# Head 0's attention operands over other tiles and through GpSimd's queue, one mLSTM stage queued behind head 0's exponentials, and a residual loaded by column range

## The chip, the cores and the metric

The kernel runs on one core of a Trainium2 chip. The profile names the core's engines: PE is TensorE (matmuls; PEld its weight loads), DVE is VectorE, ACT is ScalarE, POOL is GpSimd, and SP is SyncE, which here only issues DMAs. Each engine works through its own instructions in a fixed order, and semaphores tie the engines together: an instruction that waits holds up everything behind it on its engine. DMAs are issued from the queues of SP, ACT and POOL and run on 16 DMA engines that all queues share.

The metric is the device time of one execution in microseconds (us). A profiled execution gives a span, from the first instruction to the last, and the clock that TensorE was granted, as a share of full speed.

## The reference

The reference is one layer of a streaming encoder for a prompt of 1024 frames and a sample of 32 frames, with the same weights. All is float32. Cut to what matters here:

```python
h = x * (1 + sc1) + sh1                                  # adaLN from c
mq, mk, mv, mo, mi, mf, fq, fk, fv, ff, gu, gv = split(h @ w_in)
hm, state = mlstm(mq, mk * 64 ** -0.5, mv, mi, log_sigmoid(mf))   # 4 heads, 64-frame chunks
hm = head_norm(hm) * mlstm_norm_g * sigmoid(mo)
logits = fq @ fk.T * 64 ** -0.5 + F_q - F_k              # FoX, 8 heads, causal, F = cumsum(log_sigmoid(ff))
hf = softmax(logits) @ fv
hg = gu * (tril(ws) @ layer_norm(gv) + bs)               # gMLP over 128 frames
x = layer_norm(ALPHA * x + (1 + g1) * (concat(hm, hf, hg) @ w_o))
h = x * (1 + sc2) + sh2
y = (silu(h @ w_gate) * (h @ w_up)) @ w_down
x = layer_norm(ALPHA * x + (1 + g2) * y)
```

The outputs are x for both groups, the FoX keys, values and log forget values, the mLSTM states and the sample's gMLP rows.

## The kernel before

**Arithmetic.** A float32 product is made of three passes: each operand is split into a rounded part (hi) and the rest (lo), and TensorE adds hi x hi, hi x lo and lo x hi (`gemm`, lines 116 to 118 of the kernel). Weights come in units of 128 x 1024 by SyncE into one of three `raw` tiles (`weights`); ScalarE makes hi (line 104), VectorE makes lo (line 105).

**Stages.** Frames are columns. They are worked on in two groups, 0 to 511 and 512 to 1055 (the last 32 are the sample). First the input projections run, with the first group's share of FoX and mLSTM woven in; the results that the second group will need go out to DRAM (`dqh`, `dql` are the hi and lo parts of the scaled queries and of the keys). The region of this change follows:

1. `fm_unit` for heads 2 to 4 projects the second group's queries and keys; `evac_qk` splits them into the tiles qkh and qkl, keeps the plain keys in qkr, and stores all three.
2. `wo_mix` loads the first group's mixer outputs; `wo_res` loads the residual x of that group into the tile z0, eight row blocks of 512 columns, in four DMAs.
3. `wo_range` is the first group's output projection, once for columns 0 to 255 and once for 256 to 511, over eight weight units m. `sublayer_end` scales the result and adds the residual (line 1066); in this phase GpSimd first takes a pivot off z (line 1061). The second pass keeps the weights of the first, except m = 3 and 4. The tiles for m = 0, 1, 2 are in a pool of their own, `pw`, and m = 2 is the last of the second pass.
4. `ln1` normalises each range and writes the FFN's operand (tm_ah, tm_al); `fm_unit` for heads 5 to 7 runs beside it. For these three heads the key store leaves from ScalarE's queue.
5. `ln1_res` (line 1101, GpSimd) turns z into the FFN's residual, sixteen operations.
6. `mixers` is the second phase of FoX, for the second group's queries: for each head `fox` loads its operands (k1, k2, qp, q2 and v) and works through four tiles of 128 queries. A tile is scores (lines 779 and 780, in two PSUM banks), a mask and row maxima (782, 783), exponentials on ScalarE (788), and a scaling (796). Transposes and products with v follow (815, 823, 828). mLSTM's chunks 4 to 8 are woven in with heads 1 to 5, in stages; the first stage loads a chunk's operands and makes the output gate with three steps on ScalarE (607 to 609) and one on GpSimd (610).
7. The FFN of the first group follows in program order (`up`, `down`).

**What sets the order.** The program is traced in this order, and a planner then places each instruction on its engine by a model of the times, with earlier instructions first where several are ready. So FFN matmuls stand between the mixers' matmuls on TensorE. `issue_after(ins)` keeps instructions that are traced in its block, on the engine of `ins`, behind `ins` in that engine's order.

**Where tiles lie.** Pools opened on the right side stack downward from the top of the on-chip memory. In steps 1 to 5 the pools `p1` (the projections' operand h1 and some small tiles) and below it `sm` (the small working tiles of step 1 and earlier) stand there. They are closed before step 6, and the mixers' pool `mx1` takes the same room, beginning a little below where `sm` begins. A tile of `mx1` waits for whoever last used the tiles that it covers. In `sm` the tiles lie in the order traw, vhl, tmsum, qkr, qkh, qkl, some very small ones, gvn, gms; in `mx1` the order is k1 (two), k2, qp, q2, v, the row maxima, the probabilities, and the rest.

Of the kernel before, what the change touches and what calls it, by code (L numbers as in the profile page):

```python
# [15 lines left out]
P = 128  # L16
# [47 lines left out]
def f(ap):  # L64
    return ap.bitcast(F32)


class Kernel:
# [14 lines left out]

    def load(self, out, in_):
        self.lastload = self.nc.sync.dma_start(out, in_)
        return self.lastload
# [271 lines left out]
    def evac_qk(self, h, act=False):  # L358
        nc = self.nc

        def evac(o, n, ps):
            hi = self.t(self.sm, [P, 272], F32R, "qkh", 2)
            lo = self.t(self.sm, [P, 272], F32R, "qkl", 2)
            kr = self.t(self.sm, [P, 272], F32, "qkr", 2)
            nc.scalar.activation(hi[:, :n], ps, AF.Copy, scale=self.qsc)
            nc.vector.scalar_tensor_tensor(lo[:, :n], ps, self.qsc, f(hi[:, :n]), ALU.mult, ALU.subtract)
            if act:
                nc.scalar.activation(kr[64:, :n], ps[64:], AF.Copy)
            else:
                nc.gpsimd.tensor_tensor(kr[:, :n], f(hi[:, :n]), f(lo[:, :n]), ALU.add)  # L370
            self.store(self.dqh[h, :, o:o + n], f(hi[:, :n]))
            self.store(self.dql[h, :, o:o + n], f(lo[:, :n]))
            self.store(self.d["o_kT"][h, :, o:o + n], kr[64:, :n], nc.scalar if act else nc.gpsimd)
            if o + n == T:
                if act:
                    nc.scalar.activation(self.qks[:, h, :], ps[:, n - NS:], AF.Copy, scale=self.qsc)
                else:
                    nc.gpsimd.tensor_copy(self.qks[:, h, :], kr[:, n - NS:n])
        return evac

    def decay(self, out, h, rows, tiles):
        j0, j1 = tiles
        self.load(f(out).rearrange("p (j q) -> p j q", q=P),
                  self.dfs.rearrange("(j h) r q -> h r j q", h=8)[h, rows, j0:j1])

# [6 lines left out]
    def head_unit(self, h):  # L392
# [17 lines left out]
        for o in (0, 256):  # L410
            kr = self.t(self.sm, [P, 272], F32, "qkr", 2)
            nc.scalar.copy(kr[hi, :256], ps[hi, o:o + 256])
# [11 lines left out]
    def evac_mqk(self, i, scale):  # L424
        nc = self.nc

        def evac(o, n, ps):
            r = self.t(self.sm, [P, 272], F32, "qkr", 2)
            nc.scalar.activation(r[:, :n], ps, AF.Copy, scale=scale)
# [307 lines left out]
    def fox(self, h, chunks):  # L737
# [6 lines left out]
        else:  # L744
            k1, k2, qp, q2, v = self.head_tiles(h, nq, nk)
            qs = slice(q0, q1)
            self.load(f(qp[0:64]), self.dqh[h, 0:64, qs])
            self.load(f(qp[64:128]), self.dql[h, 0:64, qs])
            self.load(f(k1[0:64]), self.dqh[h, 64:128, :nk])
            self.load(f(k1[64:128]), self.dqh[h, 64:128, :nk])  # L750
            self.load(f(q2[0:64]), self.dqh[h, 0:64, qs])
            self.decay(q2[64:68], h, slice(2, 6), (chunks[0][0], nb))
            self.load(f(k2[0:64]), self.dql[h, 64:128, :nk])
            self.decay(k2[64:68], h, slice(0, 4), (0, nb))
            self.load(f(v), self.dv[:, :nb, h * P:(h + 1) * P])
# [5 lines left out]
    def fox_chunk(self, h, tiles, W, nq, k1, k2, qp, q2, v):  # L761
# [5 lines left out]
        for i in tiles:  # L767
# [19 lines left out]
            for x, (lo, hi) in enumerate(cuts):  # L787
                nc.scalar.activation(pr[:, lo:hi], banks[x][:, :hi - lo], AF.Exp, bias=mxs[:, 0:1],  # L788
                                     accum_out=sums[:, x:x + 1])
            if len(cuts) > 1:  # L790
# [222 lines left out]

    def wo_res(self, c, pool):
        z = self.z[c] = self.t(pool, [P, KT, GN[c]], F32, f"z{c}", 1)
        for k in range(0, KT, 2):
            self.load(z[:, k:k + 2], self.d["xT"][k:k + 2, :, GO[c]:GO[c] + GN[c]].rearrange("k p n -> p k n"))

# [24 lines left out]
    def wo_range(self, st, a, b, order, kept, pool):  # L1043
# [3 lines left out]
        for m in order:  # L1047
            self.phase = "wo0"
            w = kept.get(m) or self.weights(self.d["w_o"][m], KT, P, None, pool if m < 3 else None)
            kept[m] = w  # L1050
            ps = self.t(self.pg, [P, 512], F32, "g")
# [270 lines left out]
    def mixers(self):  # L1322
# [5 lines left out]
        for h in range(8):  # L1328
# [3 lines left out]
            if h in MLB:  # L1332
                parts.append(slow(self.mlstm(self.nextm)))
                self.nextm += 1
            weave(*parts)

    def run(self):
# [28 lines left out]
        s1 = ExitStack()  # L1366
        self.p1 = self.pool("p1", ctx=s1, side="right")
        self.sm = self.pool("sm", 2, ctx=s1, side="right")
        self.h1t = [self.wide_tiles(), [self.t(self.p1, [P, KT, GN[1]], F32R, x) for x in ("h1h", "h1l")]]
# [3 lines left out]
        self.rowp = self.t(self.cst, [P, 784], F32, "rowp")  # L1373
        self.wsp = self.t(self.p1, [P, 4, P], F32, "wsp")
        self.col = self.t(self.cst, [P, 9, 4, 4], F32, "col")
# [82 lines left out]
        self.wo_mix(0, self.KORDER[0][6:])  # L1458
        self.wo_res(0, self.pz)
        self.pn = self.pool("pn")  # L1460
# [9 lines left out]
        for h in range(PRE, 8):  # L1470
            self.fm_unit(w3[2 + h], self.evac_qk(h, True), (1,))
        self.ln1_res(0)
        s1.close()
        s4 = ExitStack()
        self.mx = self.pool("mx1", ctx=s4, side="right")
        self.foxbufs = (2, 1, 1, 1, 2)
        self.mixers()
        s5 = ExitStack()
        pa = self.pool("pa0", ctx=s5)
# [205 lines left out]
```

## Time and profile before

| | |
|---|---|
| time, median of 3 runs | 1367.51 us (1366.59 to 1367.81) |
| profiled execution, its own time | 1366.61 us |
| its span | 1364.7 us |
| granted TensorE clock, mean | 0.995 |
| TensorE busy | 1330.3 us, 97% |
| VectorE, ScalarE, GpSimd busy | 995.4, 656.7, 226.6 us |
| DMA moved | 221.70 MB, 162 GB/s on average |

How to read the rows that follow. In a row of the timeline the first number is the start in us from the span's start and the second the length; L and a number is the line of the kernel; out<-in names tiles by phase and tag; xN is the number of instructions merged; the bracket at the end tells how long the engine stood idle before and who released it. SPq, ACTq and POOLq are the queues that issue DMAs, and their lengths are those of the issue, not of the transfer. A row of waits has the time in all, how often, and the longest. In the chain of waits (followed back from the last instruction, shown in order of time) a row of DMA runs from the issue to the landing. Matmul rows overlap, since matmuls are pipelined; the distance of their starts is what one costs.

### The profile page before, as it was taken

To read this page: it belongs to the slowest core of one execution; us is meant where nothing else is said; L and a number is where in the kernel's file an instruction comes from. 1 tells how busy PE (TensorE), PEld (TensorE's weight loads), DVE (VectorE), ACT (ScalarE), POOL (GpSimd) and SP (SyncE) were. 2 spreads that over 40 slices of the span, in tenths; PEclk is the share of its full clock that TensorE was granted. 3 is DMA by queue.
4 is the path that set the end of the run, shared out by engine and by line. 5 is a ranking of instruction groups with operands and counts; after the bars stand their busy time and mean duration, and the time that the engine had idled before them with its cause. 6 is when DMAs were issued, how large, how long until landed. Compare 5 with 4: busy or idle time off the path is not lost.

```text
span 1364.7 us, 25185 instructions
## 1 busy us (share of the span) xinstructions
PE 1330.3 (97%) x9434; PEld 1215.8 (89%) x9434; DVE 995.4 (73%) x2129; ACT 656.7 (48%) x1306; POOL 226.6 (17%) x263
## 2 busy tenths in 40 slices
PE   7999999999999899999999999999999999999996
PEld 4898889998989777888887888999999999999995
DVE  5545553679769667786776765678988988879777
ACT  3314454545536554545545354336664554645355
POOL 0202000053134200000000000373710000000341
PEclk9999999999999899999999999999999999999998
DMA  9765565547454765454344334574596758454321
GB/s 359 273 231 152 161 206 154 163 138 212 134 201 135 207 189 171 119 154 134 109 122 120 104 110 130 156 181 124 164 254 170 205 149 223 146 170 127 99 79 66
DMA packets 119289, 221.70 MB, mean 162 GB/s; under 512 B 18676, under 2 KB 62352, under 8 KB 119168
## 3 DMA queue, kind: packets, MB, share of 16 engines
q1 hardware_dynamic: 111936, 207.55, 48.9%
q0 software_dynamic: 6032, 11.94, 5.1%
q8 instruction: 74, 1.21, 0.4%
q10 hardware_dynamic: 1200, 0.62, 0.2%
q14 instruction: 47, 0.39, 0.1%
HBM read 188.13 MB, written 51.85 MB: 176 GB/s over the span
## 4 chain that ended last, share of the span: by engine, by line
PE 84%; DVE 7%; DMA 5%; ACT 2%; issue 1%; SPq 1%; POOL 1%; DVEq 0%; ACTq 0%
PE up_g L117 5%; PE up_g L118 5%; PE up_g L116 5%; PE dn_g L116 4%; PE dn_g L118 4%; PE dn_g L117 4%; PE tm_g L281 3%; PE tm_g L282 3%; PE tm_g L283 3%; PE sup_u L118 3%; PE sup_u L116 3%; PE sup_u L117 3%; PE fox_t L815 2%; PE sup_g L117 2%; PE sup_g L118 2%; PE sup_g L116 2%
## 5 line engine op out<-in xcount | busy, mean ns | idle before, releaser
L117 PE MATMUL up_g<-tm_al,up_whi 128*128 128x512 f32 (+1 forms) x384 | 141.0, 367 | 0.5 <-DVE tm_al L1092 0.5
L116 PE MATMUL up_g<-tm_ah,up_whi 128*128 128x512 f32 (+1 forms) x384 | 141.2, 369 | 0.2
L118 PE MATMUL up_g<-tm_ah,up_wlo 128*128 128x512 f32 (+1 forms) x384 | 140.5, 366 | 0.0
L1211 ACT CAST sup_whi<-sup_raw 128x1024 fp32r<-128x1024 f32 x54 | 56.0, 1048 | 90.3 <-PE dn_u L117 46.7
L116 PEld LDWEIGHTS up_g<-tm_ah,up_whi 128*128 128x128 f32 x384 | 72.7, 190 | 12.5 <-ACT tm_ah L1091 0.6
L117 PEld LDWEIGHTS up_g<-tm_al,up_whi 128*128 128x128 f32 x384 | 73.1, 190 | 11.1 <-DVE tm_al L1092 0.7
L118 PEld LDWEIGHTS up_g<-tm_ah,up_wlo 128*128 128x128 f32 x384 | 73.2, 191 | 10.7
L788 ACT ACTIVATE fox_p<-fox_s,fox_fmx 128x384 f32<-128x384 f32 (+2 forms) x96 | 55.1, 578 | 44.8 <-DVE fox_fmx L786 37.4
L104 ACT CAST up_whi<-up_raw 128x1024 fp32r<-128x1024 f32 x50 | 52.4, 1048 | 49.7 <-PE up_g L117 19.0
L1212 DVE TENSOR_TENSOR sup_wlo<-sup_raw,sup_whi 128x1024 fp32r<-128x1024 f32 x54 | 68.2, 1267 | 10.5 <-ACT sup_whi L1211 10.5
L1066 DVE SCALAR_TENSOR_TENSOR wo_z<-dn_g,start_mod,wo_z 128x512 f32<-128x512 f32 (+4 forms) x120 | 60.3, 521 | 20.1 <-PE dn_g L118 19.7
L105 DVE TENSOR_TENSOR up_wlo<-up_raw,up_whi 128x1024 fp32r<-128x1024 f32 x50 | 65.7, 1314 | 11.6 <-ACT up_whi L104 11.0
L116 PE MATMUL dn_g<-up_acth,dn_whi 128*128 128x512 f32 (+2 forms) x200 | 74.1, 371 | 0.0
L118 PE MATMUL dn_g<-up_acth,dn_wlo 128*128 128x512 f32 (+2 forms) x200 | 73.4, 367 | 0.0
L117 PE MATMUL dn_g<-up_actl,dn_whi 128*128 128x512 f32 (+2 forms) x200 | 72.9, 365 | 0.0
L820 ACT CAST fox_pth<-fox_t 128x512 fp32r<-128x512 f32 (+1 forms) x80 | 41.0, 545 | 59.5 <-PE fox_t L815 59.3
L104 ACT CAST dn_whi<-dn_raw 128x1024 fp32r<-128x1024 f32 (+1 forms) x44 | 42.7, 971 | 52.2 <-PE up_g L117 10.7
L783 DVE TENSOR_REDUCE fox_fmx<-fox_s 128x1 f32<-128x384 f32 (+2 forms) x96 | 52.7, 553 | 13.0 <-PE fox_s L780 11.8
L821 DVE TENSOR_TENSOR fox_ptl<-fox_t,fox_pth 128x512 fp32r<-128x512 f32 (+1 forms) x80 | 49.5, 631 | 14.5 <-ACT fox_pth L820 14.4
L105 DVE TENSOR_TENSOR dn_wlo<-dn_raw,dn_whi 128x1024 fp32r<-128x1024 f32 (+1 forms) x44 | 49.5, 1125 | 13.7 <-ACT dn_whi L104 13.2
L281 PE MATMUL tm_g<-tm_whi,start_h1h 128*128 128x256 f32 (+1 forms) x192 | 55.3, 288 | 1.7 <-ACT tm_vhl L711 1.7
L282 PE MATMUL tm_g<-tm_wlo,start_h1h 128*128 128x256 f32 (+1 forms) x192 | 55.1, 287 | 0.0
(667 smaller groups left out, 4806.8 us busy)
## 6 DMA issues: line engine op xcount, KB each, us to landing
up_raw<-w_gu SPq DMA_DIRECT2D x50, 512.0 KB
dn_raw<-w_dn SPq DMA_DIRECT2D x28, 512.0 KB
ada_late<-w_ada SPq DMA_DIRECT2D x24, 512.0 KB
sup_raw<-w_gu SPq DMA_DIRECT2D x20, 512.0 KB
start_dp<-w_gu SPq DMA_DIRECT2D x19, 512.0 KB
start_dp<-w_gu POOLq DMA_DIRECT2D x19, 512.0 KB, 7.5
wo_raw<-w_o SPq DMA_DIRECT2D x18, 512.0 KB
sup_raw<-start_dp SPq DMA_DIRECT2D x18, 512.0 KB
```

The costliest lines, as they stand in the source:

```text
L104: nc.scalar.copy(hi[:, :w], raw[:, :w])
L105: (eng or nc.vector).tensor_tensor(lo[:, :w], raw[:, :w], f(hi[:, :w]), ALU.subtract)
L116: nc.tensor.matmul(ps, hi, xh(k), start=start and k == 0, stop=False)
L117: nc.tensor.matmul(ps, hi, xl(k), start=False, stop=False)
L118: nc.tensor.matmul(ps, lo, xh(k), start=False, stop=stop and k == n - 1)
L281: nc.tensor.matmul(ps[:, :ncol], xh, hi, start=k == 0, stop=False)
L282: nc.tensor.matmul(ps[:, :ncol], xh, lo, start=False, stop=False)
L783: nc.vector.tensor_reduce(mxs[:, x:x + 1], s[:, :w], AX.X, ALU.max, negate=True)
L788: nc.scalar.activation(pr[:, lo:hi], banks[x][:, :hi - lo], AF.Exp, bias=mxs[:, 0:1], accum_out=sums[:, x:x + 1])
L1066: self.lastz = self.nc.vector.scalar_tensor_tensor(z[:, m, x:y], ps[:, x - a:y - a], g[i], z[:, m, x:y], ALU.mult, ALU.add)
L1211: nc.scalar.copy(h, x)
L1212: tt(l, x, f(h), ALU.subtract)
```

## The change

Four parts.

1. Head 0's second phase. `load` and `decay` take an engine, and for head 0 the eight loads of qp, k1, q2 and k2 are issued by GpSimd; v stays with SyncE. The tiles qkh, qkl and qkr move from `sm` to a new pool `sq`, opened between `p1` and `sm`, and the tile wsp (gMLP's spatial weights) moves from `p1` to the start of `sm`. So `sq` lies above `sm`, and the first tiles of `mx1` cover others than before.
2. `ln1_res` is traced behind the mixers, and its GpSimd instructions queue behind the last of the loads that GpSimd issued.
3. mLSTM's chunk 4 (with head 1): its first stage is traced before head 1's weave begins, and what it has on ScalarE queues behind head 0's last exponential. The following stages come one turn earlier in the weave.
4. `wo_res` loads two row blocks of one column range. The first range's four loads come before the weights of m = 0, 2, 4, 6; the second range's queue behind the weight loads of m = 5 (blocks 0 and 4) and m = 7 (blocks 6 and 2).

```diff
-    def load(self, out, in_):
+    def load(self, out, in_, eng=None):
+        if eng:
+            self.lastside = eng.dma_start(out, in_)
+            return self.lastside
         self.lastload = self.nc.sync.dma_start(out, in_)
         return self.lastload
...
-            hi = self.t(self.sm, [P, 272], F32R, "qkh", 2)
-            lo = self.t(self.sm, [P, 272], F32R, "qkl", 2)
-            kr = self.t(self.sm, [P, 272], F32, "qkr", 2)
+            hi = self.t(self.sq, [P, 272], F32R, "qkh", 2)
+            lo = self.t(self.sq, [P, 272], F32R, "qkl", 2)
+            kr = self.t(self.sq, [P, 272], F32, "qkr", 2)
...
+            eng = self.nc.gpsimd if h == 0 else None
+            self.load(f(qp[0:64]), self.dqh[h, 0:64, qs], eng)
+            self.load(f(qp[64:128]), self.dql[h, 0:64, qs], eng)
+            self.load(f(k1[0:64]), self.dqh[h, 64:128, :nk], eng)
+            self.load(f(k1[64:128]), self.dqh[h, 64:128, :nk], eng)
+            self.load(f(q2[0:64]), self.dqh[h, 0:64, qs], eng)
+            self.decay(q2[64:68], h, slice(2, 6), (chunks[0][0], nb), eng)
+            self.load(f(k2[0:64]), self.dql[h, 64:128, :nk], eng)
+            self.decay(k2[64:68], h, slice(0, 4), (0, nb), eng)
             self.load(f(v), self.dv[:, :nb, h * P:(h + 1) * P])
...
-    def wo_res(self, c, pool):
-        z = self.z[c] = self.t(pool, [P, KT, GN[c]], F32, f"z{c}", 1)
-        for k in range(0, KT, 2):
-            self.load(z[:, k:k + 2], self.d["xT"][k:k + 2, :, GO[c]:GO[c] + GN[c]].rearrange("k p n -> p k n"))
+    def wo_res(self, a, b, k):
+        self.load(self.z[0][:, k:k + 2, a:b], self.d["xT"][k:k + 2, :, a:b].rearrange("k p n -> p k n"))
...
+            if a == 0 and m % 2 == 0:
+                self.wo_res(a, b, m)
             w = kept.get(m) or self.weights(self.d["w_o"][m], KT, P, None, pool if m < 3 else None)
+            if a == 0 and m in (5, 7):
+                with self.tc.issue_after(self.lastload.ins):
+                    for k in ((0, 4), (6, 2))[m // 7]:
+                        self.wo_res(*MM[0][1], k)
...
             if h in MLB:
-                parts.append(slow(self.mlstm(self.nextm)))
+                part = self.mlstm(self.nextm)
+                if h == 1:
+                    with self.tc.issue_after(self.lastexp.ins):
+                        next(part)
+                parts.append(slow(part))
...
         self.p1 = self.pool("p1", ctx=s1, side="right")
+        self.sq = self.pool("sq", 2, ctx=s1, side="right")
         self.sm = self.pool("sm", 2, ctx=s1, side="right")
...
-        self.wsp = self.t(self.p1, [P, 4, P], F32, "wsp")
+        self.wsp = self.t(self.sm, [P, 4, P], F32, "wsp", 1)
...
-        self.wo_res(0, self.pz)
+        self.z[0] = self.t(self.pz, [P, KT, GN[0]], F32, "z0", 1)
...
-        self.ln1_res(0)
         s1.close()
         s4 = ExitStack()
         self.mx = self.pool("mx1", ctx=s4, side="right")
         self.foxbufs = (2, 1, 1, 1, 2)
         self.mixers()
+        with tc.issue_after(self.lastside.ins):
+            self.ln1_res(0)
```

`self.lastexp` is the last exponential that `fox_chunk` traced; `head_unit` and `evac_mqk` take their qkr tile from `sq` too.

More of the change, by code (lines that the diff above doesn't have):

```diff
@@ L379, in evac_qk, with decay @@
         return evac
-    def decay(self, out, h, rows, tiles):
+    def decay(self, out, h, rows, tiles, eng=None):
         j0, j1 = tiles
         self.load(f(out).rearrange("p (j q) -> p j q", q=P),
-                  self.dfs.rearrange("(j h) r q -> h r j q", h=8)[h, rows, j0:j1])
+                  self.dfs.rearrange("(j h) r q -> h r j q", h=8)[h, rows, j0:j1], eng)
     def head_tiles(self, h, nq, nk):
@@ L410, in head_unit @@
         for o in (0, 256):
-            kr = self.t(self.sm, [P, 272], F32, "qkr", 2)
+            kr = self.t(self.sq, [P, 272], F32, "qkr", 2)
             nc.scalar.copy(kr[hi, :256], ps[hi, o:o + 256])
@@ L427, in evac @@
         def evac(o, n, ps):
-            r = self.t(self.sm, [P, 272], F32, "qkr", 2)
+            r = self.t(self.sq, [P, 272], F32, "qkr", 2)
             nc.scalar.activation(r[:, :n], ps, AF.Copy, scale=scale)
@@ L746, in fox @@
             qs = slice(q0, q1)
[L747 to L754, printed above, removed]
+            eng = self.nc.gpsimd if h == 0 else None
[7 more added lines that the diff above has]
+            self.decay(k2[64:68], h, slice(0, 4), (0, nb), eng)
             self.load(f(v), self.dv[:, :nb, h * P:(h + 1) * P])
@@ L787, in fox_chunk @@
             for x, (lo, hi) in enumerate(cuts):
-                nc.scalar.activation(pr[:, lo:hi], banks[x][:, :hi - lo], AF.Exp, bias=mxs[:, 0:1],
-                                     accum_out=sums[:, x:x + 1])
+                self.lastexp = nc.scalar.activation(pr[:, lo:hi], banks[x][:, :hi - lo], AF.Exp, bias=mxs[:, 0:1],
+                                                    accum_out=sums[:, x:x + 1])
             if len(cuts) > 1:
```

## The prediction

> **What bounds the kernel now.** I read the page first: busy time by engine, then the shares of the chain that ended last.
>
> ```profile
> span 1364.7 us, 25185 instructions
> PE 1330.3 (97%) x9434; PEld 1215.8 (89%) x9434; DVE 995.4 (73%) x2129; ACT 656.7 (48%) x1306; POOL 226.6 (17%) x263
> PE 84%; DVE 7%; DMA 5%; ACT 2%; issue 1%; SPq 1%; POOL 1%; DVEq 0%; ACTq 0%
> ```
>
> TensorE is the bound, so a change that touches none of its arithmetic can only give back time in which it waits or runs slowly. The second view is the list of TensorE's waits, for the stretch that the diff touches (340 to 470 us) and then for the stretch behind it (470 to 560).
>
> ```profile
> PE fox_s L779 <- DMA fox_k<-start_dqh: 4.2, 1, 4.2
> PE wo_g L116 <- ACT tm_ah L1003: 1.2, 1, 1.2
> PE wo_g L118 <- DVE wo_wlo L105: 1.1, 2, 0.8
> PE wo_g L116 <- ACT wo_whi L104: 0.6, 1, 0.6
> PE up_g L117 <- DVE tm_al L1092: 0.5, 1, 0.5
> ```
>
> ```profile
> PE fox_s L780 <- issue: 0.3, 1, 0.3
> ```
>
> There is one long wait, for the operands of head 0's first scores, and 2.9 us of short ones where the output projection starts. Behind 470 TensorE waits for almost nothing, so time won before is kept unless something turns late. The third view is the busy table by stretch (length, PE, PEld, DVE, ACT, POOL, granted clock, DMA share, GB/s), cut at the edges of the long wait and around the first w_o loads.
>
> ```profile
> 374.00:384.00 10.00, 8.82 (x74) 8.56 (x73) 2.93 (x6) 2.01 (x4) 2.84 (x5) 1.00 0.99 367
> 456.90:461.20 4.30, 0.07 (x1) 0.02 (x1) 0.02 (x1) 0.00 (x0) 0.91 (x2) 0.78 0.95 230
> 461.20:466.20 5.00, 4.99 (x22) 5.00 (x23) 0.54 (x3) 0.88 (x1) 0.00 (x0) 0.51 1.06 210
> ```
>
> The wait costs twice: after the 4.2 us the granted clock is 0.51 for the next 5.0 us, so 5.0 x 0.49 = 2.4 us are lost again. Between 374 and 384 the DMA engines are full (0.99).
>
> **Part 1: other tiles for head 0's operands, and another queue.** Fourth view, the issue order on SyncE's and ScalarE's queues, with SyncE's longest wait in 440 to 472:
>
> ```profile
> SPq L85 <- DMA o_kT<-fm_qkr: 3.4, 1, 3.4
> ```
>
> ```profile
> 357.86 0.37 SPq L89 DMA_DIRECT2D start_dmix<-tm_gms  x1
> 447.88 0.32 SPq L89 DMA_DIRECT2D start_dql<-fm_qkl  x1
> 449.94 0.48 ACTq L89 DMA_DIRECT2D o_kT<-fm_qkr  x1
> 454.06 0.47 SPq L85 DMA_DIRECT2D fox_qp<-start_dqh  x1
> 459.68 0.57 SPq L85 DMA_DIRECT2D fox_v<-start_dv  x1
> ```
>
> The load of qp waits for the store of the last fm_qkr, issued at 449.94 and done at about 454.0, since qp, q2 and k2 lie over qkr, qkh and qkl. By tile sizes, after the change k2 lies over traw and vhl, qp over vhl, tmsum and gvn, q2 over gvn and gms: all done by the gms store of 357.86. (The new pool begins 4.2 KB below the old one's bottom; k1 twice 4 KB, then k2 4, qp 2, q2 2, v 4. The old one held 2 KB of traw, 4 of vhl, 1 of tmsum, then the six tiles of 1.06 KB that now move out, gvn 2, gms 2; wsp's 2 KB now come first.) v (16 KB above the pool's start) still lies over qkr and qkh, which is where it leaves SyncE's queue as now. k1 stays over the last kept w_o tile, read by the second range's matmuls to 425.0. Next rows: that limit, where the first FFN matmul follows the last projection, what DMA issues on GpSimd cost (min/median/max) and take to land, and GpSimd's arithmetic.
>
> ```profile
> L117 PE MATMUL wo_g<-tm_al,wo_whi x128: 276/281/467, 374.3 to 425.0; 128*128 128x256 f32 x128
> 444.63 0.28 PE L116 MATMUL up_g<-tm_ah,up_whi 128*128 128x256 f32 x1
> L1163 POOL DMA_DIRECT2D start_dp<-w_gu x19: 1023/1030/1569, 902.5 to 1203.1; - x19
> L89 POOL DMA_DIRECT2D o_kT<-fm_qkr x10: 521/546/751, 119.6 to 380.2; - x10
> start_dp<-w_gu POOLq DMA_DIRECT2D x19, 512.0 KB, 7.5
> o_kT<-fm_qkr POOLq DMA_DIRECT2D x10, 68.0 KB, 4.7
> L1101 POOL TENSOR_SCALAR wo_z<-wo_z,start_colp x32: 549/760/3413, 422.6 to 982.4; 128x256 f32<-128x256 f32 x16, 128x272 f32<-128x272 f32 x16
> ```
>
> Eight loads from 425.0: at 0.5 us each the last issue ends at 429.2, at 1.57 us at 437.6; landing 4.7 to 7.5 us later, 434 to 445. I take 1.03 us (these are 8 to 256 KB, between the two rows) and 7.5: 440.7, that is before TensorE leaves the projections at 444.6. So the wait goes: -4.2. What TensorE does in its place is the rest of the FFN's first unit, which now runs from 461.9 to 466.2: its last operand, tm_al, is written at 456.9 (row below), so it can follow at once, and at full clock: -2.4. Without that cover, with ln1 later, TensorE would stand for each us that tm_al is late. SyncE's queue sheds eight issues between 454.06 and 459.68; v and what follows go up to 5.6 us earlier. I count that as zero, as nobody waits there afterwards, with +-1.3 at the ends.
>
> What is late next is the softmax. Head 0's row maxima and first probability tile still lie over qkh and qkl, whose last store is issued at 447.88; with the 4.1 us that the o_kT store took (449.94 to 454.0) that is 452. From then on head 0's VectorE work meets ln1's second range, which paces the FFN's first unit:
>
> ```profile
> 455.98 0.95 DVE L1092 TENSOR_TENSOR tm_al<-lna_tmp,tm_ah 128x256 fp32r<-128x256 f32 x2
> 466.28 0.56 DVE L783 TENSOR_REDUCE fox_fmx<-fox_s 128x1 f32<-128x384 f32 x1 [0.53 <-PE fox_s L780]
> 466.82 0.29 DVE L782 TENSOR_TENSOR fox_s<-fox_s,start_maskneg 128x128 f32<-128x128 f32 x1
> 471.22 0.55 DVE L796 TENSOR_SCALAR fox_p<-fox_p,fox_fsm 128x640 f32<-128x640 f32 x1
> ```
>
> One score tile takes two reductions (0.56, the second at most that), a mask (0.29), three operations on single columns, each at most a mask's time, and the scaling (0.55): at most 2 x 0.56 + 4 x 0.29 + 0.55 = 2.8 us. Put wholly ahead of ln1's end at 456.9 that is +2.8, behind it 0. I take +1.2, a little under half, since ln1 comes first in program order.
>
> **Part 2: ln1_res.** Its 16 GpSimd operations move behind the last side load: median 0.76, so 12 us, at most 16 x 3.4 = 55 us from 438. The first reader is the first down projection:
>
> ```profile
> L1066 DVE SCALAR_TENSOR_TENSOR wo_z<-dn_g,start_mod,wo_z x120: 233/490/753, 519.7 to 1349.3; 128x512 f32<-128x512 f32 x40, 128x272 f32<-128x272 f32 x24, 128x240 f32<-128x240 f32 x24, 128x32 f32<-128x32 f32 x24
> ```
>
> The late end is 493 and the reader comes at 519.7, or some 8 us earlier, so 0. Behind them on GpSimd queue only mLSTM's two memsets and one multiply. Without that cover each us late is a us at the first down projection.
>
> **Part 3: mLSTM's chunk 4.** Its first stage comes one turn earlier in program order, but its three ScalarE steps queue behind head 0's last exponential.
>
> ```profile
> 470.03 0.41 ACT L607 ACTIVATE mlstm_mo<-mlstm_mo 128x256 f32<-128x256 f32 x1
> 472.21 0.41 ACT L609 ACTIVATE mlstm_mo<-mlstm_mo 128x256 f32<-128x256 f32 x1
> ```
>
> Three steps of some 0.4 us, 1.3 us, leave the first softmax's way. Their product is used at the chunk's end only, so nobody waits. TensorE waits 0.3 us in this stretch, so the gain is between 0 and 0.3; a loss up to 1.3 if the block lands before another exponential. I take 0.
>
> **Part 4: residual by range.** The rows of 371 to 396, SyncE's queue and one link of the chain, and GpSimd's first use in the second range:
>
> ```profile
> 371.34 3.41 SPq L85 DMA_DIRECT2D wo_z<-xT  x4
> 386.34 9.67 SPq L85 DMA_DIRECT2D wo_raw<-w_o  x4
> ```
>
> ```profile
> 375.76 9.63 DMA wo_raw<-w_o
> ```
>
> ```profile
> 408.44 7.64 POOL L1061 TENSOR_TENSOR wo_z<-wo_z,wo_pv 128x256 f32<-128x256 f32 x7 [14.20 <-ACT wo_pv L929]
> ```
>
> Today four loads of 512 KB, 2 MB, go ahead of a w_o load that then takes 9.63 us. Only half of it, 1 MB, stays ahead: at the 367 GB/s of that stretch the weights land 2.9 us earlier. The waits for whi and wlo (0.6 + 1.1) go: -1.7. The wait for tm_ah (1.2) hangs on a mixer load in the same crowd: between 0 and -1.2, I take -0.6. The other 1 MB follows the loads of w_o 5 and 7: if the last issue is at 396.0 and takes 9.63 us it is there at 405.6, before 408.44. The count of issues rises from 4 to 8, 0.4 us each or so, hidden under the DMA.
>
> **The sum.** -4.2 - 2.4 + 1.2 - 1.7 - 0.6 = -7.7. The profiled execution took 1366.61 (span 1364.7 and 1.9 around it): 1358.9. The median of the three runs, 1367.51, is 0.9 above it, so on that footing 1359.8. With every term at its better end, -4.2 - 2.4 - 1.7 - 1.2 - 1.3 = -10.8: 1356.7; at its worse, -4.2 - 2.4 + 2.8 + 1.3 = -2.5: 1365.0.
>
> **The rivals.** *A, the weights hold it.* In 469 to 498 the chain runs through the FFN weights, one load after another:
>
> ```profile
> 469.07 6.64 DMA up_raw<-w_gu
> ...
> 476.81 1.22 DVE up_wlo L105
> ```
>
> ```profile
> 480.79 0.40 PE L118 MATMUL up_g<-tm_ah,up_wlo 128*128 128x512 f32 x1
> ```
>
> The low part is ready at 478.03 and used at 480.79: 2.8 us of room. If these loads do not move up, TensorE arrives at most 2.8 us earlier, plus the 1.7 of part 4: -4.5, 1363.0. Against it: the load at 469.07 waits for a buffer which TensorE's own progress frees, so it shifts along.
>
> *B, the wait changes place.* Scores take two banks each tile; the exponentials that free them cannot start before 452. If the planner puts the second tile's scores ahead of the FFN's matmuls, TensorE stands where it stood and only part 4 stays: -1.7, 1365.8.
>
> *C, the other side: GpSimd is late.* Its arithmetic stretches from 0.55 to 3.41 us beside a busy VectorE. Eight issues stretched to 3.41: 425.0 + 27.3 + 7.5 = 459.8. The scores, planned for 444.6 at the head of the FFN, then hold TensorE 15.2 us instead of 4.2: +11.0 - 2.3 = +8.7, 1376. It decides from a landing after 451.2 (444.6 + 6.6), where part 1 gives nothing. Against it: the issues, unlike the arithmetic, never took over 1.57.
> The Trainium skill, page "SBUF — State Buffer", section "SBUF: two separate sides", states this one: a DMA from GpSimd's queue has its descriptors written by GpSimd's cores, which are shut out while VectorE holds the port pair that they share. By that rule the change would go C's way; the issue rows above do not show it so far.
>
> **How the numbers follow.** The sum 0.58, A 0.13, B 0.13, C 0.16. About 0.2%, 2.7 us, is what a measurement can tell here: faster means under 1364.8. The sum and most of A are faster, 0.68; B and a rest 0.14; C and reorderings behind 470 that I cannot see, 0.18. The range goes from the better end of the sum, 1356.5, over A and B to 1369.0; C and the tails stay out. The likeliest case alone has 1356.7 to 1365.0.
>
> **What would show it.** Right: no wait of L779 for fox_k, a granted clock of 1.00 through 450 to 470, eight loads on GpSimd's queue between 425 and 440, the FFN's first 512-wide matmul near 458.5 instead of 466.21 (less the 7.7), no waits for wo_whi. Wrong: a new wait of fox_s or fox_t between 440 and 500 (B, C), of up_g for up_wlo (A), or of wo_g for wo_z (part 4).

## The result, and the profile after

The changed kernel takes 1370.48 us (median of 20 runs, 1367.15 to 1374.52) against 1366.15 for the kernel before (20 runs): ratio 1.003, 95% interval 1.0022 to 1.0038. By that ratio it is 4.1 us slower (the medians differ by 4.3), where 7.7 us faster was forecast. The profiled execution took 1368.07 (span 1365.2 and 2.9 around it), 2.4 us below the median; a second profile of the same kernel took 1371.76 and has a span of 1369.9. Much of the difference between these two is there before the projection starts (374.15 and 377.06), so below each stretch is measured inside its own trace.

Lines of the changed kernel stand 3 to 8 lower in the file than before: L104 is L107, L615 is L618, L779 is L783, L1092 is L1100, L1101 is L1109. First the list of TensorE's waits in the changed kernel, for 340 to 440 us, 440 to 470 and 470 to 560:

```profile
PE wo_g L119 <- ACT tm_ah L1007: 0.7, 1, 0.7
PE wo_g L119 <- ACT wo_qs L940: 0.5, 1, 0.5
```

```profile
PE ada_g L187 <- ACT ada_adas L184: 2.0, 1, 2.0
PE up_g L120 <- DVE tm_al L1100: 1.4, 1, 1.4
PE up_g L119 <- DVE up_sil L1150: 1.2, 2, 1.0
```

```profile
PE fox_o L827 <- DVE fox_ptl L825: 1.2, 1, 1.2
```

The wait of 4.2 us for fox_k is gone, and so are those for whi and wlo. In their place stand waits for adas, tm_al and up_sil in 440 to 470, and for fox_ptl behind 470; of these the kernel before has tm_al's alone, with 0.5. The busy table by stretch (columns as in the prediction) shows where:

```profile
446.00:448.00 2.00, 1.99 (x17) 1.78 (x16) 2.00 (x4) 1.95 (x7) 2.00 (x2) 1.00 0.20 70
448.00:450.00 2.00, 0.57 (x2) 0.37 (x3) 2.00 (x6) 2.00 (x6) 2.00 (x2) 1.00 0.50 109
450.00:452.00 2.00, 1.01 (x7) 0.80 (x7) 1.70 (x4) 1.79 (x5) 2.00 (x5) 1.00 0.82 261
452.00:454.00 2.00, 2.00 (x11) 2.00 (x11) 1.88 (x6) 1.72 (x5) 2.00 (x3) 0.54 0.94 259
454.00:456.00 2.00, 2.00 (x16) 1.78 (x16) 0.87 (x3) 0.28 (x1) 2.00 (x3) 0.61 1.11 220
...
460.00:462.00 2.00, 0.24 (x2) 0.00 (x0) 1.32 (x2) 1.78 (x6) 0.00 (x0) 1.00 0.73 212
462.00:464.00 2.00, 1.57 (x4) 1.03 (x5) 1.46 (x7) 0.88 (x3) 0.00 (x0) 0.60 0.97 308
464.00:466.00 2.00, 2.00 (x7) 1.56 (x6) 0.29 (x1) 0.00 (x0) 0.00 (x0) 0.55 0.72 295
```

There are two gaps, 448 to 452 (1.43 + 0.99 us without a matmul) and 460 to 464 (1.76 + 0.43), and each has a stretch near half clock behind it. Before, there was one long gap with one such stretch. The timeline of VectorE, ScalarE and SyncE's queue shows what holds the second gap (start, length, engine, line, operation; in brackets the idle time before it and what ended it):

```profile
453.49 0.42 SPq L88 DMA_DIRECT2D mlstm_mb<-start_dM  x1
459.49 0.69 DVE L618 TENSOR_TENSOR mlstm_mw<-mlstm_mb,start_maskbig 128x512 f32<-128x512 f32 x1 [4.62 <-DMA mlstm_mb<-start_dM]
460.22 1.28 ACT L621 ACTIVATE mlstm_mw<-mlstm_mw,start_col 128x128 f32<-128x128 f32 x4 [1.08 <-DVE mlstm_mw L618]
461.40 0.49 ACT L1148 ACTIVATE up_sil<-up_sil,start_ones 128x256 f32<-128x256 f32 x1
461.81 0.35 ACT L184 COPY ada_adas<-ada_g 128x256 f32<-128x256 f32 x1
```

mLSTM chunk 4's second stage (L618, then four exponentials) now stands in the middle of the FFN's first unit. VectorE stood idle in order for 4.62 us there, because the load of mb, issued at 453.49, lands some 6 us later on DMA engines that are full (share 0.94 and 1.11 in the rows above). The exponentials follow, and behind these on ScalarE is the copy of adas for which TensorE waits. Before, the same instruction came after head 0's maxima and cost little:

```profile
470.02 0.69 DVE L615 TENSOR_TENSOR mlstm_mw<-mlstm_mb,start_maskbig 128x512 f32<-128x512 f32 x1 [0.66 <-DMA mlstm_mb<-start_dM]
```

Its load of mb left SyncE's queue at 466.11 then, 12.6 us later than now:

```profile
466.11 0.33 SPq L85 DMA_DIRECT2D mlstm_mb<-start_dM  x1
```

GpSimd, on the other hand, did what was forecast, and earlier: the loads leave between 413.7 and 423.9, not after 425. Those of qp follow GpSimd's last pivot operation at once, and k1 comes free at 420.62, 2.5 us before the projection ends, so it seems not to lie over the tile that is read last.

```profile
413.74 0.55 POOL L86 DMA_DIRECT2D fox_qp<-start_dqh  x1
420.62 1.03 POOL L86 DMA_DIRECT2D fox_k<-start_dqh  x2 [5.81 <-PE wo_g L121]
423.29 0.64 POOL L86 DMA_DIRECT2D fox_k<-start_dfs  x1
442.81 14.47 POOL L1109 TENSOR_SCALAR wo_z<-wo_z,start_colp 128x256 f32<-128x256 f32 x16
```

The time of all traces can be cut at three points that every kernel has: the start of the first and the end of the last matmul of the first output projection, and the start of the first one of the second projection (near 877). For the middle stretch the busy table gives TensorE's busy time, here before and changed:

```profile
425.38:877.44 452.06, 446.72 (x2526) 377.33 (x2527) 321.97 (x679) 229.76 (x484) 31.84 (x37) 0.99 0.49 140
```

```profile
423.15:878.42 455.27, 449.47 (x2528) 377.39 (x2526) 325.97 (x679) 230.43 (x484) 32.12 (x40) 0.99 0.47 138
```

Length less busy time is idle. The loss by half clock is busy time x (1 - granted clock), summed over slices of 2 us. What is left is called work here; TensorE counts as busy in it, at full clock.

| kernel | projection | middle stretch | idle | half clock | work | rest |
|---|---|---|---|---|---|---|
| before | 51.20 | 452.06 | 5.35 | 2.46 | 444.25 | 487.26 |
| changed | 49.00 | 455.27 | 5.79 | 3.00 | 446.48 | 486.78 |
| changed, second profile | 49.17 | 457.01 | 6.23 | 4.69 | 446.09 | 486.66 |

Part 4's gain is there (-2.0 to -2.2) and the rest is the same. The middle stretch lost 3.2 to 5.0 us: idle and half clock, which part 1 was to reduce, are no smaller, and the work takes 1.8 to 2.2 us more.

### The profile page after: what moved, and what is told of

The parts are those of the page before. It is cut to its first block, busy times and chain, and to the rows that moved or that the text cites. A ratio compares the mean times of both kernels' runs of the same rounds, so it can differ in the third digit from the quotient of the medians.

```text
span 1365.2 us, 25201 instructions
## 1 busy us (share of the span) xinstructions
PE 1333.0 (98%) x9434; PEld 1215.8 (89%) x9434; DVE 998.5 (73%) x2129; ACT 657.9 (48%) x1306; POOL 227.1 (17%) x271
## 4 chain that ended last, share of the span: by engine, by line
PE 86%; DVE 5%; DMA 5%; ACT 2%; issue 1%; SPq 1%; ACTq 0%; DVEq 0%
PE up_g L119 5%; PE up_g L121 5%; PE up_g L120 5%; PE dn_g L121 4%; PE dn_g L119 4%; PE dn_g L120 4%; PE tm_g L284 3%; PE tm_g L285 3%; PE tm_g L286 3%; PE sup_u L121 3%; PE sup_u L119 3%; PE sup_u L120 3%; PE fm_g L119 2%; PE fox_t L819 2%; PE wo_g L121 2%; PE wo_g L119 2%
## 5 line engine op out<-in xcount | busy, mean ns | idle before, releaser
L107 ACT CAST up_whi<-up_raw 128x1024 fp32r<-128x1024 f32 x50 | 52.4, 1049 | 55.6 <-PE up_g L120 23.9
L108 DVE TENSOR_TENSOR up_wlo<-up_raw,up_whi 128x1024 fp32r<-128x1024 f32 x50 | 67.1, 1342 | 11.0 <-ACT up_whi L107 10.2
L107 ACT CAST dn_whi<-dn_raw 128x1024 fp32r<-128x1024 f32 (+1 forms) x44 | 42.7, 972 | 52.4 <-PE up_g L120 11.6
L108 DVE TENSOR_TENSOR dn_wlo<-dn_raw,dn_whi 128x1024 fp32r<-128x1024 f32 (+1 forms) x44 | 49.5, 1125 | 15.0 <-ACT dn_whi L107 14.4
```

The costliest lines, as they stand in the source:

```text
L107: nc.scalar.copy(hi[:, :w], raw[:, :w])
L108: (eng or nc.vector).tensor_tensor(lo[:, :w], raw[:, :w], f(hi[:, :w]), ALU.subtract)
```

## The experiments

My theory after this reading: part 4 is a gain by itself, and the loss comes with part 1's other queue. With eight issues gone from SyncE's queue the planner expects mLSTM's loads early and puts its steps ahead of the FFN's first unit. The rivals were part 3 (which traces mLSTM's first stage earlier), part 2 (GpSimd's sixteen operations run through ln1's second range), and the order behind 500.

**Each part alone or away.** `only_part4` is the kernel before with the residual by range:

```diff
-        self.wo_res(0, self.pz)
+        self.z[0] = self.t(self.pz, [P, KT, GN[0]], F32, "z0", 1)
+            if a == 0 and m % 2 == 0:
+                self.wo_res(a, b, m)
...
```

> The kernel before with the residual by range alone (part 4); the other three parts undone. Theory (the loss comes with the loads' other queue, and part 4 is a gain by itself): the second FFN's order is as before, so the output projection ends 1.5 to 2.5 us earlier and the whole kernel is 1.5 to 2.5 us faster, ratio 0.998 to 0.999. Rival (part 4 carries the loss, its eight loads or their late half colliding with the weights): 2 us or more slower, ratio above 1.001.

Measured: 0.9978 (0.9963 to 0.9992), 3.0 us faster. The projection takes 49.08 in place of 51.20. Part 4 is a gain by itself. The wait for fox_k is 3.0 in it, since the load of qp now waits only 1.1 us for the store of o_kT.

`only_part1` has the other tiles and GpSimd's loads, with ln1_res and mLSTM in their old places:

```diff
-            kr = self.t(self.sm, [P, 272], F32, "qkr", 2)
+            kr = self.t(self.sq, [P, 272], F32, "qkr", 2)
+            eng = self.nc.gpsimd if h == 0 else None
-            self.load(f(qp[0:64]), self.dqh[h, 0:64, qs])
+            self.load(f(qp[0:64]), self.dqh[h, 0:64, qs], eng)
...
```

> The kernel before with the other tiles and GpSimd's loads alone (part 1); ln1_res, mLSTM's chunk and the residual as before. Theory (once the eight loads have left SyncE's queue, the planner takes the mLSTM's block for ready and puts mLSTM's L618 and the memset of foxs_k ahead of the FFN's first unit on VectorE, where they stand and wait): the wait for fox_k is gone, waits for up_sil and ada_adas of together 5 us or more come in 445 to 470 with two stretches near half clock, and the kernel is 2 to 7 us slower than before, ratio 1.0015 to 1.005. Rival 1 (part 3 is what does it): no such waits, 4 to 6 us faster, ratio 0.9955 to 0.997. Rival 2 (part 2 does it): likewise faster, ratio below 0.998.

Measured: 1.0086 (1.006 to 1.0112), 11.8 us slower, worse than any theory said. The wait that I expected gone is longer, and the new ones are there too:

```profile
PE fox_s L783 <- DMA fox_k<-start_dqh: 6.3, 1, 6.3
PE ada_g L187 <- ACT ada_adas L184: 1.5, 1, 1.5
PE up_g L120 <- DVE tm_al L1096: 1.3, 1, 1.3
```

`no_part2` and `no_part3` are the changed kernel with that part undone:

```diff
+        self.ln1_res(0)
         s1.close()
...
-        with tc.issue_after(self.lastside.ins):
-            self.ln1_res(0)
```

> The changed kernel without part 2: ln1_res in its old place on GpSimd, so that 11 of its 16 operations stand ahead of the eight loads. Theory: the second gap near 460 stays, the first one near 450 may shrink by up to 1.5 us as VectorE's ln1 is less disturbed; ratio 1.001 to 1.004. Rival 2 (GpSimd's sixteen operations through ln1's second range are the cause): both gaps shrink, 3 us or more faster than the changed kernel, ratio 0.997 to 1.001. If the loads now come too late behind those operations, a wait for fox_k or fox_qp of several us comes back and the ratio is above 1.004.

Measured: 1.0071 (1.0049 to 1.0092), 9.7 us slower than before and 5.6 slower than the changed kernel. The last clause of the expectation came true. GpSimd's queue in this run:

```profile
447.01 4.74 POOL L1109 TENSOR_SCALAR wo_z<-wo_z,start_colp 128x256 f32<-128x256 f32 x3 [12.27 <-ACT lna_tmp L1095]
451.69 0.59 POOL L86 DMA_DIRECT2D fox_qp<-start_dqh  x1
453.85 1.08 POOL L86 DMA_DIRECT2D fox_k<-start_dqh  x2
```

With ln1_res ahead of them the loads leave 33 to 38 us later than in the changed kernel, and the wait for fox_k is 6.3 us here as well. So part 2 is what makes part 1's queue early, and is worth 5.6 us. Not all of that is the wait for fox_k: L618 stands for the load of mb 9.65 us in this run, in place of 4.62. Whether GpSimd's operations disturb ln1 stays open: without part 2 TensorE waits 0.7 us for tm_al here and 1.3 in only_part1, against 1.4 in the changed kernel.

```diff
-                part = self.mlstm(self.nextm)
-                if h == 1:
-                    with self.tc.issue_after(self.lastexp.ins):
-                        next(part)
-                parts.append(slow(part))
+                parts.append(slow(self.mlstm(self.nextm)))
```

> The changed kernel without part 3: mLSTM's chunk 4 is traced where it was, not ahead of head 1. Theory: nothing is won, L618 still stands ahead of the FFN's first unit and waits for the load of mb; ratio to before 1.001 to 1.005, as for the changed kernel (1.003). Rival 1 (part 3 is the cause): the second gap near 460 goes, 4 to 7 us faster than the changed kernel, ratio 0.996 to 0.999.

Measured: 1.0024 (1.0011 to 1.0036), the same as the changed kernel. Undoing part 3 does not help, so it isn't the cause. In this run two engines stand for a load of mLSTM's, ScalarE for the first stage's (mo) and VectorE for the second's (mb), and TensorE waits 4.6 us for adas behind them:

```profile
460.28 0.42 ACT L610 ACTIVATE mlstm_mo<-mlstm_mo 128x256 f32<-128x256 f32 x1 [4.67 <-DMA mlstm_mo<-start_dmo]
460.94 0.69 DVE L618 TENSOR_TENSOR mlstm_mw<-mlstm_mb,start_maskbig 128x512 f32<-128x512 f32 x1 [4.75 <-DMA mlstm_mb<-start_dM]
```

Counted in the traces, the mask of mLSTM's chunk 4 (L615 or L618) is the 784th instruction of VectorE in the kernel before and in only_part4, and the 773rd in only_part1, no_part2, no_part3 and the changed kernel: it moves with part 1.

**Tiles or queue.** `tiles_syncq` is only_part4 with part 1's tiles, the loads left on SyncE:

```diff
+        self.sq = self.pool("sq", 2, ctx=s1, side="right")
         self.sm = self.pool("sm", 2, ctx=s1, side="right")
...
-            kr = self.t(self.sm, [P, 272], F32, "qkr", 2)
+            kr = self.t(self.sq, [P, 272], F32, "qkr", 2)
...
-        self.wsp = self.t(self.p1, [P, 4, P], F32, "wsp")
+        self.wsp = self.t(self.sm, [P, 4, P], F32, "wsp", 1)
```

> The kernel before with part 4 and the other tiles of part 1, but with head 0's eight loads left on SyncE's queue and ln1_res and mLSTM in their old places, so that the order of every engine is that of only_part4. Theory (the tiles alone carry part 1's gain, and the other queue its loss, since only that lets the planner move mLSTM's L618 up): the loads no longer wait for the store of o_kT (3.4 us) and the wait for fox_k (3.0 in only_part4) shrinks under 1 us, most of the half clock behind it goes; 2 to 5 us faster than only_part4, ratio 0.994 to 0.9965. Rival (the loads are held by DMA traffic, not by the tiles): the wait for fox_k stays at 2 us or more, ratio as only_part4's 0.998.

Measured: 0.999 (0.9976 to 1.0005), not faster than only_part4. Neither side's numbers came: the wait for fox_k shrinks to 1.3, with no half clock behind it, but TensorE's list for 480 to 900 now begins with

```profile
PE fox_o L827 <- DVE fox_ptl L825: 1.1, 1, 1.1
PE fox_t L819 <- DVE fox_p L800: 1.1, 1, 1.1
```

and one of 0.5 for up_wlo. What was won is given back 20 to 40 us later. The tiles alone are worth nothing measurable, and L618 stays the 784th instruction: it is the queue that moves it.

**The suspected step itself.** `changed_again` is the changed kernel, on the chip of the next two:

> The changed kernel itself, beside the next three on the same chip. Expected: ratio 1.002 to 1.004 as before, and in its profile the two gaps of TensorE at 448 to 452 and 460 to 463, each with a stretch near half clock behind it; whether the two stretches at half clock are there in each profile or not is open.

Measured: 1.0027 (1.0016 to 1.0039); both gaps are there, and both stretches at half clock. `hold_mlstm` queues the second stage behind head 0's softmax:

```diff
-                nc.vector.tensor_scalar(pr[:, :n], pr[:, :n], sums[:, 0:1], None, ALU.mult)
+                self.lastsc = nc.vector.tensor_scalar(pr[:, :n], pr[:, :n], sums[:, 0:1], None, ALU.mult)
...
+                    part = self.held(part, self.lastsc.ins, self.lastexp.ins)
...
+    def held(self, part, sc, ex):
+        with self.tc.issue_after(sc), self.tc.issue_after(ex):
+            next(part)
+        yield
+        yield from part
```

> The changed kernel with mLSTM chunk 4's second stage (L618 on VectorE, the four exponentials L621 on ScalarE) queued behind head 0's last scaling and last exponential. Theory (L618 waits in order for the late load of mb, and holds up_sil, ada_adas and head 0's maxima behind it): the gap of TensorE near 460 to 463 goes, with the half clock behind it, some 2.2 + 1.5 us; ratio to before 0.999 to 1.001, 3 to 5 us faster than the changed kernel. Rival (the loss lies behind 500, where the planner's other order makes the heads 3 to 12 us later): the gap goes and the time stays, ratio 1.002 to 1.004.

Measured: 0.9967 (0.9954 to 0.998), 4.5 us faster than before and 8.2 to 8.6 faster than the changed kernel, twice what I had expected of it. So the loss hangs on where this stage stands. It stands later than in the kernel before now, as the 836th instruction; its old place together with GpSimd's queue was not tried. The rows of hold_mlstm for the two gaps:

```profile
448.00:450.00 2.00, 0.82 (x5) 0.42 (x3) 2.00 (x5) 2.00 (x7) 2.00 (x2) 1.00 0.36 59
450.00:452.00 2.00, 0.97 (x6) 0.77 (x6) 1.70 (x4) 2.00 (x7) 2.00 (x4) 0.98 0.82 249
452.00:454.00 2.00, 1.79 (x8) 1.79 (x9) 2.00 (x6) 1.53 (x5) 2.00 (x3) 0.50 0.83 243
...
460.00:462.00 2.00, 1.66 (x11) 1.08 (x8) 1.55 (x6) 0.94 (x3) 0.00 (x0) 1.00 0.95 291
462.00:464.00 2.00, 2.00 (x11) 1.58 (x10) 0.59 (x2) 0.15 (x1) 0.00 (x0) 1.00 0.74 224
```

The second gap is gone (0.34 us left), the first stays. Only part of the gain can be placed in the traces. Against the two profiles of the changed kernel the middle stretch is 6.1 and 7.9 us shorter: some 3.2 and 3.6 of this are the second gap with the half clock behind it, 1.2 and 1.6 the wait for fox_ptl, 0.3 and 1.5 half clock behind the first gap, and 1.5 and 1.2 are work, whose cause is open.

`hold_and_memset` also takes one memset from VectorE to GpSimd:

```diff
-            nc.vector.memset(kc[64:66], 1.0)
+            (nc.vector if g else nc.gpsimd).memset(kc[64:66], 1.0)
```

> The same, and the first memset of foxs_k on GpSimd ahead of ln1_res instead of on VectorE amid ln1's second range. Theory: the first gap near 448 to 452 shrinks by the memset's 0.9 us, and where the half clock behind it goes too, by up to 2.5 us; ratio 0.997 to 1.000. Rival (GpSimd's sixteen operations, which run through the same stretch, make ln1 late, not the memset): the first gap stays within 0.5 us, ratio as in the run that holds mLSTM alone.

Measured: 0.9964 (0.995 to 0.9978), by time the same as hold_mlstm. In the trace the wait for up_sil (1.3) is gone and that for tm_al (1.4) stays; idle time falls from 2.76 to 1.45. So the memset's 0.91 us is about a third of the first gap. Whether GpSimd's sixteen operations make the rest was not tried by itself. The record has a hint: VectorE's rows just ahead of tm_al (L1092 twice, L108, then L1092 three times) take 0.95, 1.41 and 1.28 us in hold_mlstm, which has all sixteen run from 443.26 on, and 0.76, 1.22 and 1.09 in no_part2, which has three of them here, from 447.01 on: some 0.6 us less in all.

`mb_first` changes what L618 waits for, not its place: the load of mb goes first of mLSTM's loads.

```diff
+        if j == 4:
+            qb, v, mo, mb = (t([P, 2, 2, P], "mqb"), t([P, 4, 65], "mv1", 1), t([P, 256], "mo", 1), t([P, 4, P], "mb", 1))
+            self.load(mb[:L, :, :L], self.dM[4 * j:4 * j + 4, :L].partition_broadcast(L))
         self.load(qk[:, :, :L], self.dmqk[:, :, o:o + L])
...
```

> The changed kernel with mLSTM chunk 4's load of mb issued first of its loads, some four issues earlier on SyncE's queue; VectorE's order is the same through its 700th row, L618 (here L625) still ahead of the FFN's first unit. Theory (L618 stands for the load of mb): the load leaves some 2 us earlier, L618 starts 2 us or so earlier, the second gap shrinks by 1.5 to 2.5 us, and the kernel is 1 to 5 us faster than the changed one, ratio to before 0.999 to 1.002. Rival (its place in the order costs, whatever it waits for; or the crowded DMA engines land it no earlier): second gap and time unchanged, ratio 1.002 to 1.004.

Measured: 1.0 (0.999 to 1.0009), some 4 us faster than the changed kernel. L618, here L625:

```profile
458.68 0.69 DVE L625 TENSOR_TENSOR mlstm_mw<-mlstm_mb,start_maskbig 128x512 f32<-128x512 f32 x1 [2.76 <-DMA mlstm_mb<-start_dM]
```

It waits 2.76 in place of 4.62 us. The second gap, though, did not shrink as I had said. It grew: TensorE waits 3.0 us for adas in this trace, in place of 2.0. The middle stretch is 453.47, and shorter mainly because no half clock follows the first gap and the work is less. That L618 stands for mb is shown; that its wait is what this run gained by is not.

**What each other part is worth once the stage is held.** `hold_no_part3` traces the first stage where it was, with no queueing behind head 0's exponentials; the second stage stays held:

```diff
-                    with self.tc.issue_after(self.lastexp.ins):
-                        next(part)
                     part = self.held(part, self.lastsc.ins, self.lastexp.ins)
...
     def held(self, part, sc, ex):
+        next(part)
+        yield
         with self.tc.issue_after(sc), self.tc.issue_after(ex):
```

> hold_mlstm with mLSTM chunk 4's first stage back in its old place (part 3 undone), the second stage still queued behind head 0's softmax. Theory (part 3 is worth nothing either way): ratio as in hold_mlstm, 0.995 to 0.998. Rival (part 3 keeps three ScalarE steps out of head 0's way, which now shows): 1 to 2 us slower than hold_mlstm, ratio 0.9975 to 0.999.

Measured: 0.9999 (0.9987 to 1.0011), 4.4 us slower than hold_mlstm, more than even the rival said. The same thing happens, on another engine:

```profile
460.81 0.42 ACT L610 ACTIVATE mlstm_mo<-mlstm_mo 128x256 f32<-128x256 f32 x1 [6.32 <-DMA mlstm_mo<-start_dmo]
```

ScalarE stands for the load of mo, and TensorE waits 3.6 us for adas behind it. So part 3 guards against exactly this stall, for the first stage only. In the changed kernel the second stage stands in its place, and in no_part3 both stand at the same time (the two rows above), so undoing part 3 by itself adds nothing.

`hold_no_part4` is hold_mlstm with the residual loaded whole:

```diff
-        self.z[0] = self.t(self.pz, [P, KT, GN[0]], F32, "z0", 1)
+        self.wo_res(0, self.pz)
...
```

> hold_mlstm without part 4: the residual loaded whole ahead of the projection, as before. Theory (part 4 is a gain of its own, 2 to 3 us, that adds to the rest): ratio 0.998 to 0.9995, the projection's first range 2 us longer. Rival (part 4's gain is taken up by ln1 when the loads of head 0 are out of the way): ratio as in hold_mlstm, 0.9955 to 0.9975.

Measured: 0.9985 (0.9972 to 0.9997), 2.5 us slower than hold_mlstm, with the projection at 51.04. Part 4's gain adds to the others'.

All profiles, cut as above:

| kernel | ratio | projection | middle stretch | idle | half clock | work |
|---|---|---|---|---|---|---|
| only_part4 | 0.9978 | 49.08 | 449.99 | 4.05 | 1.67 | 444.27 |
| tiles_syncq | 0.999 | 49.11 | 450.41 | 4.98 | 0.00 | 445.43 |
| only_part1 | 1.0086 | 49.86 | 460.83 | 11.32 | 2.54 | 446.96 |
| no_part2 | 1.0071 | 48.56 | 462.40 | 11.98 | 3.93 | 446.49 |
| no_part3 | 1.0024 | 48.35 | 456.24 | 7.12 | 1.57 | 447.55 |
| hold_mlstm | 0.9967 | 48.84 | 449.15 | 2.76 | 1.45 | 444.94 |
| hold_and_memset | 0.9964 | 48.74 | 447.32 | 1.45 | 0.00 | 445.87 |
| mb_first | 1.0 | 48.44 | 453.47 | 6.50 | 1.70 | 445.27 |
| hold_no_part3 | 0.9999 | 48.83 | 454.75 | 6.15 | 3.80 | 444.80 |
| hold_no_part4 | 0.9985 | 51.04 | 447.59 | 2.41 | 0.00 | 445.18 |

Open: the last column. It is 1.0 to 3.3 us above before's where L618 stands early, and 0.6 to 1.6 where it is held, with no wait in the lists to account for it (tiles_syncq, with L618 in its old place, is 1.2 above). The chain that ended last does not tell them apart: from 478 to 518 it runs through the FFN weights in the changed kernel and not in hold_mlstm, but in the kernel before, where the work is least, it runs through them as well, from 469 to 495.

## Why the prediction was wrong

**Part 4, -1.7 and -0.6: right.** 2.1 us in the projection of only_part4, 2.5 to 3.0 in time. The waits for whi and wlo went as said; tm_ah kept 0.7 of its 1.2, and 0.5 for wo_qs came.

**The wait for fox_k, -4.2: right, but only with part 2.** I counted part 2 as 0 and began the loads at 425.0, as if nothing stood ahead of them on GpSimd. That held in the changed kernel and hid that part 2 makes it hold: without it the loads go to 452 to 457. The size was right; that it rests on part 2 was not in the working.

**The half clock, -2.4: wrong.** It left its place and came back at two others, 3.00 and 4.69 us in the two profiles. I had tied it to the one long wait; after shorter gaps it comes as well.

**Head 0's VectorE work ahead of ln1, +1.2: wrong work, and too small.** Head 0's maxima came later than before (469.86 against 466.28), not ahead of ln1. What does stand amid ln1 is the memset of foxs_k (0.91). The first gap is 2.42 us in hold_mlstm, with 1.45 of half clock behind it, against 0.77 and nothing in only_part4: +3.1 in place of +1.2. This fits that parts 1 to 3, with mLSTM held, bring only some 1.5 us over part 4 alone (0.9967 against 0.9978, with overlapping intervals).

**SyncE's relief, 0 with +-1.3 at the ends, "as nobody waits there afterwards": the step that failed.** I asked who waits for SyncE's queue, and not what is planned by it. With eight issues less on that queue, L618 stands eleven instructions further up in VectorE's order, ahead of work on TensorE's path, and waits there 4.62 us for a load that lands some 6 us after its issue. That the queue moves it is shown by tiles_syncq. That the planner does so because it expects mLSTM's loads earlier is my reading of its rule; no profile shows what it expects. Holding the stage back gives 8.2 to 8.6 us (changed kernel against hold_mlstm); the wait itself, with what it does to TensorE and its clock, makes 3.2 to 3.6 of them, and the rest comes with the other order, in part without a wait that the lists show. In the prediction's own words for part 3, "nobody waits" for mLSTM's product, which holds for the product and not for the instructions queued behind its making.

**Part 3, 0: right as measured, for the wrong reason.** By itself it changes nothing (1.0024 against 1.003), with the second stage held it is worth 4.4 us. I looked only at three steps of 0.4 us out of the softmax's way; what counts is the load that the first of them waits for.

**The rivals.** B's words, that the wait changes place, fit, but the score banks had no part in it. A's chain through the weights is there again behind 470. C's price, 1376, is what no_part2 takes (1376.55), which is a coincidence: there arithmetic stands ahead of the loads, and no issue is stretched. In the changed kernel they take 0.52 to 0.64 us each, while VectorE was busy for 16.84 of the 20 us in which most of them fall:

```profile
420.00:440.00 20.00, 20.00 (x158) 19.80 (x158) 16.84 (x39) 15.20 (x38) 3.30 (x6) 1.00 0.70 193
```

The rule of the Trainium skill, page "SBUF — State Buffer", section "SBUF: two separate sides", that GpSimd cannot write descriptors while VectorE holds the shared ports, is not seen in these issues: none took over 0.64 us, below the 0.75 that the kernel before shows at most for its ten, and they landed 4.0 to 7.1 us after their issue. They don't disprove it either, as the page ties it to VectorE's two-port modes, and the trace does not show which mode an instruction ran in.

Put together: the forecast was -7.7. hold_mlstm, the change with that one stage held back, is at -4.5, 1361.95 us; the 8.2 to 8.6 us that go with L618's early place turn this into +4.1. Of the 3.2 us between -7.7 and -4.5 the first gap makes 1.9 (+3.1 in place of +1.2); the rest is not placed.

## What to carry to other kernels

When instructions leave a queue, ask which work becomes ready sooner in the planner's eyes, and where it will stand in the order of engines that run strictly in order: an instruction whose result nobody needs soon can still block the ones behind it while its own operand is on the way. Hold such work behind the stretch that paces the kernel, all its stages and not the first alone. And price a part together with the others that it relies on: part 2 was worth nothing in my sum and 5.6 us on the chip.

## What was unexpected of the hardware

The granted clock falls after gaps shorter than I had taken it to need, and not each time. In the changed kernel 2.42 us of idle time, nearly all of it in two waits of 1.4 and 1.0 us with 1.0 us of matmuls between them, were followed by clocks of 0.54 and 0.61. The run without part 3 has the same two waits (2.43 us idle in the rows below) and keeps the full clock:

```profile
448.00:450.00 2.00, 1.71 (x13) 1.30 (x11) 2.00 (x4) 1.95 (x6) 2.00 (x2) 1.00 0.21 74
450.00:452.00 2.00, 0.86 (x6) 0.77 (x6) 1.73 (x5) 2.00 (x7) 2.00 (x3) 1.00 0.83 203
452.00:454.00 2.00, 1.00 (x8) 0.89 (x8) 1.97 (x5) 1.52 (x5) 2.00 (x4) 1.00 0.85 258
454.00:456.00 2.00, 2.00 (x22) 1.57 (x21) 1.88 (x6) 1.61 (x5) 2.00 (x3) 1.00 0.92 235
```

Seven profiles have this gap with 2.0 us or more and parts 1 and 2 in place. Four show the fall (both of the changed kernel, hold_mlstm, hold_no_part3) and three do not (no_part3, mb_first, hold_no_part4). The Trainium skill, page "TensorE: Matmul & The Clock Gate", Part 1, says that activity is watched in a free-running window of some 3.4 us and that the effect varies from run to run with its phase; the traces agree as far as nearly the same waits end both ways, but they do not show the phase. Single waits divide more clearly: those of 1.9 us and more (the second gap of the changed kernel with 1.97 and 1.90, fox_k in only_part4 with 2.96, adas in mb_first with 3.00) were each followed by the fall, and those of 1.32 in tiles_syncq and 1.40 in hold_and_memset were not. So a gap of some 2 us in two pieces costs nothing more in one profile and another 1.5 to 3.0 us in the next, and a single profile does not tell which. Whether one kernel can go both ways is not shown: the only one with two profiles here, the changed kernel, fell in both.
